# Output products of a two-stage layer: operand sums made inside the plain group, a last evacuation deferred, tiles padded

## The chip, the core and the metric

The kernel runs on one core of a Trainium2 chip. The metric is the device time of one execution in microseconds (us). Five engines matter: TensorE (PE; its weight loads are the row PEld), VectorE (DVE), ScalarE (ACT), GpSimd (POOL), and SyncE (SP), which issues the DMAs. Each works through its own list of instructions in order; a semaphore wait on the first one holds up all behind it.

## The reference

The input x has 512 tokens of 2048 features, all float32. One layer of a gated recurrence (HGRN2), then one of forgetting attention (FoX), each with a gate path and an output product added to the stream:

```
def hgrn2_layer(x, norm_w, w_in, lb, out_norm_w, w_out):
    h = rmsnorm(x, norm_w)
    proj = h @ w_in
    ...
    o = o.reshape(B, T, D_MODEL) * jax.nn.silu(gate.astype(jnp.float32))
    return x + (o.astype(x.dtype) @ w_out)
```

The attention layer ends in the same way: the branch times silu(gate), a product with a 2048 x 2048 matrix, and the residual. These two output products are what the change is about.

## The kernel before

Everything is kept transposed: a tile is 128 features by 512 tokens, and a 2048-wide operand is 16 contraction tiles (kt). Every product is made from operands split into a high part (a cast on ScalarE, line L432) and a low part (a subtraction on DVE, L433), with three matmuls: high by high, high by low, low by high.

**A plain group** (group, L205) makes four output tiles in four PSUM banks gm: for each kt it takes one weight tile wh, wl (128 x 512) and issues 4 x 3 matmuls of 512 columns (L227 to L229, with Xh and Xl moving; in the token-major form L223 to L225 the weights move and x is stationary). Weights come by DMA in chunks of 512 KB (tile wr, two buffers, two kt each). At each kt, group splits the weights of the next kt ahead of the matmuls; at the last kt that is the first weight of the *next* group. In stages A and B, split weights have three buffers, in the output stages two (w_tiles, L124).

**A quick group** (quick, L254) makes two output tiles of 512 tokens with seven products where eight would be needed, a Strassen-Winograd scheme: for each of eight pairs p of contraction tiles it issues seven products of 256 columns, three matmuls each (L282 to L284). Both operands then need sums: those of the weights (w_sums, L142, tile wm, DVE L146 to L148) for each weight chunk, and those of the input (quick_prep, L239), made once for all six quick groups of a stage. For a pair, quick_prep takes four quarters of two y tiles, makes three differences on DVE (L244, L246, L247) and one on POOL (L245) in the single buffer tm, and splits them: one over the upper half of Xh[p], Xl[p] (256 columns), three into th, tl (768 columns). The upper half of Xh[p] may be overwritten only when the plain group has read it. quick_sum (L287) takes the seven products apart: one ScalarE copy (L291), seven DVE operations (L292 to L301), and the result is stored, squared and added to the norm's sum (x1_done, ScalarE L346, POOL L347).

**The stages.** a: sixteen plain groups (order_a, the last is g3), with the recurrence's small tasks in between; oa: the output product, one plain group for output tiles 0 to 3 and six quick groups u0 to u5 for the other twelve; b and ob likewise, the first group of b is q0. A gate group ends with gate_evac (L374): for each of four banks a DVE product z (L378), on ScalarE Abs, Exp, Ln and Exp (L364 to L366, L381), on DVE L367, on POOL z times t (L382), on DVE y times z (L384). y is the input of the output product and is split per kt (y_split) as xh, xl.

**Pools.** Each stage has its own tile pool (phase, L67), all laid over the same addresses, so a tile of a new stage waits for the last readers of what lay there. Which instruction stands where in an engine's list is set by a scheduler that goes by the order of the program's lines and a timeline of its own; the lists shown below are its result.

**What surrounds the change.** out_product (L823) runs the plain group first, still in the pool of the old stage with three weight buffers: while g3's last contraction tiles are on TensorE, its first weights are already split. Only at its last kt are the remaining tasks flushed and the new phase opened; the sums of pairs 0 to 3 are then issued, those of 4 to 7 inside u0. Pair p is the contraction tiles p and p + 8. After oa's u5 its evacuation is issued at once, then phase b is opened, the small forget-gate weights wf, wfs are made (L852 to L858), and q0 begins, whose x1_split (L846) splits the rows of x1 one kt after the other.

Of the kernel before, what the change touches and what calls it, by code (L numbers as in the profile page):

```python
# [1 line left out]

# [29 lines left out]
def hgrn2_fox(ctx, tc, io):  # L32
# [10 lines left out]

    def nt(tag, shape, bufs, dt=F32, pool=None):
        uid[0] += 1
        return (pool or sb).tile(list(shape), dt, tag=tag, name=f"{tag}_{uid[0]}", bufs=bufs)

    def const(tag, shape, dt=F32):
        return cp.tile(list(shape), dt, tag=tag, name=tag)

    def view(t, offset, dims):
        return bass.AP(t.tensor, t.offset + offset, [t.ap[0], *dims])
# [7 lines left out]
    def bank():  # L60
        return nt("mx", (P, T), 4, pool=ps)
# [96 lines left out]
    class Chunks:  # L158
# [43 lines left out]
        Xl[kt] = nt(f"xl{kt}", (P, T), 1, F32R)  # L202
        return Xh[kt], Xl[kt]

    def group(evac, token_major=False, rate=3, before=None):  # L205

        banks = [nt(f"gm{j}", (P, T), 1, pool=ps) for j in range(4)]
        for kt in range(KT):
            if kt % 2 == 0:
                wts.load()  # L210
            if before:
                before(kt)
            if not wts.parts:
                wts.split()
            h, l = wts.take()
            if not wts.parts:
                wts.split()
            for j in range(4):
                c = slice(j * P, (j + 1) * P)
                f, e = kt == 0, kt == KT - 1  # L220
                if token_major:
                    xh, xl = Xh[kt][:, c], Xl[kt][:, c]
                    PE.matmul(banks[j], xh, h, start=f, stop=False)  # L223
                    PE.matmul(banks[j], xh, l, start=False, stop=False)  # L224
                    PE.matmul(banks[j], xl, h, start=False, stop=e)  # L225
                else:
                    PE.matmul(banks[j], h[:, c], Xh[kt], start=f, stop=False)  # L227
                    PE.matmul(banks[j], h[:, c], Xl[kt], start=False, stop=False)  # L228
# [9 lines left out]

    def quick_prep(p, y):  # L239

        kt = p + KT // 2
        b11, b12, b21, b22 = y[p][:, :TN], y[p][:, TN:], y[kt][:, :TN], y[kt][:, TN:]
        m = mt("tm", (P, 4, TN), 1)
        V.tensor_sub(m[:, 0, :], b12, b11)  # L244
        G.tensor_sub(m[:, 2, :], b12, b22)  # L245
        V.tensor_sub(m[:, 1, :], b22, m[:, 0, :])  # L246
        V.tensor_sub(m[:, 3, :], b21, m[:, 1, :])  # L247
        th = mt(f"th{p}", (P, 3, TN), 1, F32R)
        tl = mt(f"tl{p}", (P, 3, TN), 1, F32R)
        split(m[:, 0, :], Xh[p][:, TN:], Xl[p][:, TN:])  # L250
        split(m[:, 1:4, :], th, tl)
        return th, tl

    def quick(banks, prep, evac, before=None):  # L254

        half = lambda i: banks[i // 2][:, (i % 2) * TN : (i % 2 + 1) * TN]
        for p in range(KT // 2):
            if p % 2 == 0:
                wts.load()
# [12 lines left out]
            for i, (a, xh, xl) in enumerate((
                (2, Xh[p][:, lo], Xl[p][:, lo]),
                (5, th[:, 0, :], tl[:, 0, :]),
                (1, th[:, 2, :], tl[:, 2, :]),
                (3, Xh[p][:, hi], Xl[p][:, hi]),
                (0, Xh[kt][:, lo], Xl[kt][:, lo]),
                (6, Xh[kt][:, hi], Xl[kt][:, hi]),
                (4, th[:, 1, :], tl[:, 1, :]),
            )):  # L280
                o = half(i)
                PE.matmul(o, h[:, a, :], xh, start=f and i % 2 == 0, stop=False)  # L282
                PE.matmul(o, h[:, a, :], xl, start=False, stop=False)
                PE.matmul(o, l[:, a, :], xh, start=False, stop=e and (i % 2 == 1 or i == 6))  # L284
        evac(*banks)

    def quick_sum(r1, r2, o1, o2, p16, p45, p23, p7):  # L287

# [11 lines left out]
        V.tensor_add(o1, e, r1)  # L300
        V.tensor_add(o2, d, r2)  # L301

    def quick_groups(y, residual, evac):

        prep = [quick_prep(p, y) for p in range(4)]

        def run():
            for u in range(6):
                k = 4 + 2 * u
                r = [residual(k), residual(k + 1)]  # L310
                banks = [nt(f"gm{j}", (P, T), 1, pool=ps) if u % 2 == 0 else bank() for j in range(4)]
                quick(
                    banks, prep, lambda *p, k=k, r=r: evac(k, r, p),
                    before=(lambda p: p < 4 and prep.append(quick_prep(4 + p, y))) if u == 0 else None,
                )

        return run


    def sum_parts(x, out_bank):  # L320
# [13 lines left out]
    class Norm:  # L334
# [15 lines left out]
        def finish(self):  # L350
            b = bank()
            sum_parts(self.acc, b)
            self.row = nt("rstd", (P, T), 1)
            rsqrt_mean(self.row, b, D)
            b2 = bank()
            for w in range(NW):
                PE.transpose(b2[:, w * P : (w + 1) * P], self.row[:, w * P : (w + 1) * P], ident)
            self.col = nt("rstdc", (P, NW, 1), 1)
            V.tensor_copy(self.col, b2.rearrange("p (w c) -> p w c", c=P)[:, :, 0:1])


# [9 lines left out]
    def gate_evac(norm, h0):  # L371
        def evac(j, bk):
            h = h0 + j
            new = Y[h] is None  # L374
            if new:
                Y[h] = nt(f"y{h}", (P, T), 1)
            z = Y[h] if new else nt("z", (P, T), 4)
            V.tensor_mul(z, bk, norm.row)  # L378
            l = tmp()
            log_sigmoid(l, z, l)  # L380
            S.activation(l, l, AF.Exp)  # L381
            G.tensor_mul(z, z, l)  # L382
            if not new:
                V.tensor_mul(Y[h], Y[h], z)  # L384

        return evac
# [373 lines left out]
    for name in order_a:  # L760
        kind, i = name[0], int(name[1])
        before = load_x if name == order_a[0] else None
        if kind == "q":
            group(qf_evac(2 * i), before=before, rate=RATE_A)
            tasks.append((2 * i, mix_a(2 * i)))
            tasks.append((2 * i + 1, mix_a(2 * i + 1)))
        elif kind == "v":
            group(v_evac(norm0, 4 * i), token_major=True, rate=RATE_A)
        else:
            group(gate_evac(norm0, 4 * i), rate=RATE_A)  # L770

# [80 lines left out]
    wf = mt("t", (P, KT, H), 4)  # L852
    nc.sync.dma_start(wf, io["wb_f"])
    wfs = mt("wfs", (P, KT, 48), 1, F32R)
    V.memset(wfs.bitcast(F32), 0.0)
    V.tensor_mul(wf, wf, view(nk, 0, [[1, KT], [0, H]]))
    V.tensor_copy(wfs[:, :, 0:H], wf)
    V.tensor_sub(wfs[:, :, 32 : 32 + H], wf, rd(wfs)[:, :, 0:H])  # L858
    f_d = dr.tile([H, T], F32, tag="fd", name="fd")

    def forget():
# [108 lines left out]
    for name in order_b:  # L970
        kind, i = name[0], int(name[1])
        if kind == "q":
            group(qk_evac(2 * i), before=x1_split if first else None, rate=RATE_B)
            if first:
                forget()
            first = False
            tasks.append((2 * i, mix_b(2 * i)))
            tasks.append((2 * i + 1, mix_b(2 * i + 1)))
        elif kind == "v":
            group(v_evac(norm1, 4 * i), token_major=True, rate=RATE_B)  # L980
        else:
            group(gate_evac(norm1, 4 * i), rate=RATE_B)

    def res_b(kt):
        r = nt("z", (P, T), 4)
# [14 lines left out]
        for i in range(2):  # L1000
            nc.sync.dma_start(io["out"][k + i], r[i])

    out_product(out_b_evac(), res_b, quick_b, RATE_B, "ob")
    cur["ctx"].close()


# [75 lines left out]
```

## Time and profile before

| quantity | value |
|---|---|
| time, median of 3 runs | 2089.97 us (2087.96 to 2094.06) |
| time of the profiled execution | 2092.97 us |
| its span, first to last instruction | 2091.2 us |
| mean granted TensorE clock | 0.989 |
| TensorE busy | 2028.2 us, 97% |
| VectorE busy | 1579.0 us, 76% |
| ScalarE busy | 1132.6 us, 54% |
| GpSimd busy | 316.1 us, 15% |
| DMA | 195.01 MB, mean 93 GB/s |

How to read the rows that follow. A row of stretches gives from:to in us, its length, then for each engine the busy time and the count of instructions, the mean granted TensorE clock (1.00 is full), the busy share of the DMA engines and GB/s. A row of waits gives who waits for whom, the total in us, how often, and the longest. A row of a tile or a line gives the count and durations in ns. A timeline row gives start, duration, engine, line, operation, output <- inputs, and in brackets how long the engine was idle before it and what ended that. The duration of a matmul includes its way through the array; how fast they follow each other is seen from their starts or their count in a stretch. Line numbers are those of the kernel before.

### The profile page before, as it was taken

To read this page: it belongs to the slowest core of one execution; us is meant where nothing else is said; L and a number is where in the kernel's file an instruction comes from. 1 tells how busy PE (TensorE), PEld (TensorE's weight loads), DVE (VectorE), ACT (ScalarE), POOL (GpSimd) and SP (SyncE) were. 2 spreads that over 40 slices of the span, in tenths; PEclk is the share of its full clock that TensorE was granted. 3 is DMA by queue.
4 is the path that set the end of the run, shared out by engine and by line. 5 is a ranking of instruction groups with operands and counts; after the bars stand their busy time and mean duration, and the time that the engine had idled before them with its cause. 6 is when DMAs were issued, how large, how long until landed. Compare 5 with 4: busy or idle time off the path is not lost.

```text
span 2091.2 us, 28900 instructions
## 1 busy us (share of the span) xinstructions
PE 2028.2 (97%) x10202; PEld 1701.7 (81%) x10202; DVE 1579.0 (76%) x3250; ACT 1132.6 (54%) x2312; POOL 316.1 (15%) x404
## 2 busy tenths in 40 slices
PE   7999999999999999988989999999999999999798
PEld 5888888888888888768977888888888888888698
DVE  8778977988799788769884667665766666685887
ACT  5646655666566465634443555554555556564343
POOL 7303210322132031211210000010001000011100
PEclk9999999999999999989999999999999999999899
DMA  5222222222222222233533232223222222223353
GB/s 172 81 81 81 71 81 71 81 81 71 81 71 81 76 76 71 90 117 117 161 104 91 87 95 91 86 78 99 91 86 87 91 91 86 86 82 109 101 165 108
DMA packets 61408, 195.01 MB, mean 93 GB/s; under 512 B 7872, under 2 KB 8000, under 8 KB 61264
## 3 DMA queue, kind: packets, MB, share of 16 engines
q1 hardware_dynamic: 61120, 193.17, 29.5%
q8 instruction: 80, 1.31, 0.3%
q14 instruction: 64, 0.52, 0.1%
q10 hardware_dynamic: 144, 0.01, 0.0%
HBM read 184.73 MB, written 8.42 MB: 92 GB/s over the span
## 4 chain that ended last, share of the span: by engine, by line
PE 83%; DVE 7%; DMA 3%; ACT 2%; issue 2%; POOL 2%; SPq 0%; DVEq 0%; ACTq 0%; POOLq 0%
PE gm L227 17%; PE gm L229 17%; PE gm L228 17%; PE gm L224 5%; PE gm L223 5%; PE gm L225 5%; DVE wl L433 3%; DMA wr<-in_wb_q 2%; PE mx L580 1%; PE mx L579 1%; PE mx L578 1%; PE mx L427 1%; PE mx L428 1%; PE mx L284 1%; PE mx L426 1%
## 5 line engine op out<-in xcount | busy, mean ns | idle before, releaser
L227 PE MATMUL gm<-xh,wh 128*128 128x512 f32 x1664 | 662.0, 398 | 13.9 <-ACT wh L432 8.3
L228 PE MATMUL gm<-xl,wh 128*128 128x512 f32 x1664 | 661.8, 398 | 0.0
L229 PE MATMUL gm<-xh,wl 128*128 128x512 f32 x1664 | 625.6, 398 | 5.7 <-DVE wl L433 5.5
L227 PEld LDWEIGHTS gm<-xh,wh 128*128 128x128 f32 x1664 | 314.3, 189 | 86.5 <-ACT wh L432 8.3
L229 PEld LDWEIGHTS gm<-xh,wl 128*128 128x128 f32 x1664 | 312.1, 189 | 77.6 <-DVE wl L433 7.0
L228 PEld LDWEIGHTS gm<-xl,wh 128*128 128x128 f32 x1664 | 314.5, 189 | 71.6
L432 ACT CAST wh<-wr 128x512 fp32r<-128x512 f32 (+1 forms) x336 | 217.3, 649 | 232.5 <-PE gm L228 125.8
L433 DVE TENSOR_TENSOR wl<-wr,wh 128x512 fp32r<-128x512 f32 (+1 forms) x336 | 261.8, 783 | 107.7 <-ACT wh L432 101.5
L138 DVE SCALAR_TENSOR_TENSOR wl<-wr,v_b_norm_w,wh 128x256 fp32r<-128x256 f32 (+1 forms) x192 | 113.7, 594 | 152.1 <-ACT wh L137 141.2
L137 ACT ACTIVATE wh<-wr,v_b_norm_w 128x256 fp32r<-128x256 f32 (+1 forms) x192 | 111.9, 586 | 196.8 <-PE gm L228 155.9
L224 PE MATMUL gm<-wl,xh 128*128 128x512 f32 x512 | 203.7, 398 | 0.4 <-DVE wl L433 0.4
L225 PE MATMUL gm<-wh,xl 128*128 128x512 f32 x512 | 202.1, 396 | 0.0
L223 PE MATMUL gm<-wh,xh 128*128 128x512 f32 x512 | 185.8, 396 | 0.0
L137 ACT ACTIVATE wh<-wr,v_kv_norm_w 128x256 fp32r<-128x256 f32 (+1 forms) x192 | 110.3, 575 | 63.2 <-PE gm L225 46.2
L138 DVE SCALAR_TENSOR_TENSOR wl<-wr,v_kv_norm_w,wh 128x256 fp32r<-128x256 f32 (+1 forms) x192 | 111.2, 580 | 38.6 <-ACT wh L137 38.0
L924 POOL TENSOR_SCALAR_AFFINE_SELECT s<-s 128x128 f32<-128x128 f32 x64 | 27.4, 428 | 669.7 <-DVE s L923 669.0
L573 DVE COPY_PREDICATED at<-m,mx 128x128 f32<-128x128 uint8 (+3 forms) x448 | 106.6, 296 | 13.6 <-PE mx L580 13.0
L223 PEld LDWEIGHTS gm<-wh,xh 128*128 128x128 f32 x512 | 95.9, 188 | 22.4 <-DVE q L544 0.2
L224 PEld LDWEIGHTS gm<-wl,xh 128*128 128x128 f32 x512 | 96.2, 188 | 21.5 <-DVE wl L433 0.9
L225 PEld LDWEIGHTS gm<-wh,xl 128*128 128x128 f32 x512 | 96.1, 188 | 20.9
L432 ACT CAST kh<-k 128x512 fp32r<-128x512 f32 (+1 forms) x96 | 56.4, 587 | 52.0 <-PE mx L579 25.8
L382 POOL TENSOR_TENSOR z<-z,t 128x512 f32<-128x512 f32 x32 | 47.9, 1509 | 237.0 <-ACT t L381 236.9
(217 smaller groups left out, 3893.9 us busy)
## 6 DMA issues: line engine op xcount, KB each, us to landing
wr<-in_wa_qf SPq DMA_DIRECT2D x64, 512.0 KB, 3.6
wr<-in_wb_qk SPq DMA_DIRECT2D x64, 512.0 KB, 3.5
wr<-in_wa_v SPq DMA_DIRECT2D x32, 512.0 KB, 3.5
wr<-in_wa_g SPq DMA_DIRECT2D x32, 512.0 KB, 3.5
wr<-in_wb_v SPq DMA_DIRECT2D x32, 512.0 KB, 3.5
wr<-in_wb_g SPq DMA_DIRECT2D x32, 512.0 KB, 3.5
wr<-in_wa_q SPq DMA_DIRECT2D x24, 512.0 KB, 3.6
wr<-in_wb_q SPq DMA_DIRECT2D x24, 512.0 KB, 3.6
```

Of the source, the lines that this page charges most:

```text
L137: S.activation(h[:, c], r[:, c], AF.Copy, scale=w[:, kt : kt + 1])
L138: V.scalar_tensor_tensor(l[:, c], r[:, c], w[:, kt : kt + 1], rd(h)[:, c], op0=ALU.mult, op1=ALU.subtract)
L223: PE.matmul(banks[j], xh, h, start=f, stop=False)
L224: PE.matmul(banks[j], xh, l, start=False, stop=False)
L225: PE.matmul(banks[j], xl, h, start=False, stop=e)
L227: PE.matmul(banks[j], h[:, c], Xh[kt], start=f, stop=False)
L228: PE.matmul(banks[j], h[:, c], Xl[kt], start=False, stop=False)
L229: PE.matmul(banks[j], l[:, c], Xh[kt], start=False, stop=e)
L382: G.tensor_mul(z, z, l)
L432: S.copy(h, src)
L433: return V.tensor_sub(l, src, rd(h))
L573: V.copy_predicated(out, mv, data)
```

## The change

Four things are altered.

1. **The output stages** open their phase before the plain group instead of at its last kt. The sums of a pair are made inside the plain group, as soon as both of its y tiles have been split, that is after each odd kt.
2. **Pairs** are neighbouring contraction tiles, 2p and 2p + 1, instead of p and p + 8; the host lays the weights of the quick groups out accordingly. The count of instructions on each engine stays the same.
3. **hold** keeps the last gate group of a stage, and u5 of oa, from splitting the first weight of the following group. quick returns its evacuation as a function; oa's last one is called inside q0 at its third kt, and the forget-gate weights are made at its seventh.
4. **Padding**: a tile whose rows aren't a multiple of 64 bytes is made longer, so that every tile begins at a multiple of 64 bytes. Before, all tiles of the stages' pools began 32 bytes beyond one; xh, xl, y, z and wr lie in another pool that began at a multiple already. A small tile (rstdc) goes to the pool of constants.

```
     def quick_prep(p, y):
-        kt = p + KT // 2
-        b11, b12, b21, b22 = y[p][:, :TN], y[p][:, TN:], y[kt][:, :TN], y[kt][:, TN:]
+        k1, k2 = 2 * p, 2 * p + 1
+        b11, b12, b21, b22 = y[k1][:, :TN], y[k1][:, TN:], y[k2][:, :TN], y[k2][:, TN:]
...
-    def out_product(evac0, residual, evac, rate, name):
-
-        rest = []
+    def out_product(evac0, residual, evac, name, hold):
+
+        flush()
+        phase(name)
+        prep = []
 
         def before(kt):
             y_split(kt)
-            if kt == KT - 1:
-                flush()
-                phase(name)
-                rest.append(quick_groups(Yd, residual, evac))
-
-        group(evac0, before=before, rate=rate)
-        rest[0]()
-
-    out_product(out_a_evac(), res_a, quick_a, RATE_A, "oa")
+            if kt % 2:
+                prep.append(quick_prep(kt // 2, Yd))
+
+        group(evac0, before=before)
+        return quick_groups(prep, residual, evac, hold)
+
+    last_a = out_product(out_a_evac(), res_a, quick_a, "oa", True)
...
     def x1_split(kt):
+        if kt == 2:
+            last_a()
+        if kt == 6:
+            forget_weights()
...
-            if not wts.parts:
+            if not (wts.parts or hold and kt == KT - 1):
                 wts.split()
...
-        b = w.reshape(2, 8, P, n, 2, P).transpose(3, 1, 2, 0, 4, 5)
+        b = w.reshape(8, 2, P, n, 2, P).transpose(3, 0, 2, 1, 4, 5)
```

What that does to the engines' lists, at three places. In the changed kernel the lines of group, quick and the splits lie some further down (L432 is L435, L227 is L237, L378 is L381, L364 to L366 are L367 to L369, L381 is L384, L384 is L387). The numbers behind a name tell buffers apart.

**ScalarE, from the end of g3 into oa's plain group, before.** wh_9232 and wh_9323 are the plain group's weights of kt 0 and 1, t the gate activations of g3's last evacuation:

```order
L432 CAST wh_9216<-wr_9180 128x512 [waits DVE_50,PE_50]
L432 CAST wh_9232<-wr_9214 128x512 [waits DMAHW1_50,DVE_50,PE_50]
L432 CAST wh_9323<-wr_9214 128x512 [waits DVE_50,PE_50]
L364 ACTIVATE t_9241<-z_9239 128x512 [waits DVE_50]
L432 CAST wh_9343<-wr_9317 128x512 [waits DMAHW2_50,PE_50,Activation_50]
L364 ACTIVATE t_9254<-z_9252 128x512 [waits DVE_50]
L365 ACTIVATE t_9241<-t_9241 128x512 [waits Activation_50]
```

The weights go ahead of the activations. **The same place after the change;** here wh_9323 and wh_9327 are kt 0 and 1:

```order
L369 ACTIVATE t_9276<-t_9276 128x512 [waits Activation_50]
L384 ACTIVATE t_9250<-t_9250 128x512 [waits DVE_50]
L384 ACTIVATE t_9263<-t_9263 128x512 [waits DVE_50]
L384 ACTIVATE t_9276<-t_9276 128x512 [waits DVE_50]
L435 CAST xh_1878_9641<-y_1426_7294 128x512 [waits DVE_50,PE_50]
L435 CAST xh_1882_9661<-y_1502_7684 128x512 [waits DVE_50,PE_50]
L435 CAST xh_1890_9694<-y_1619_8290 128x512 [waits DVE_50,PE_50]
L435 CAST wh_9323<-wr_9214 128x512 [waits DMAHW1_50,Pool_50]
L435 CAST wh_9327<-wr_9214 128x512 [waits PE_50]
```

All sixteen activations and the casts of y tiles 12 to 14 now stand ahead of the first weight, and that waits for POOL: its buffer lies over t_9276, which POOL reads in its last product. Stage ob has the same pattern.

**DVE, inside oa's plain group, after the change.** wl are low weights, tm, tl and the 256-wide xl belong to the sums (before, this stretch held low weights and xl only):

```order
L436 TENSOR_TENSOR xl_1819_9377<-tm_9400,xh_1818_9376 128x256 [waits Activation_50]
L254 TENSOR_TENSOR tm_9453<-y_622_3138 128x256 [waits DVE_50]
L256 TENSOR_TENSOR tm_9453<-y_698_3528,tm_9453 128x256 [waits DVE_50]
L257 TENSOR_TENSOR tm_9453<-y_698_3528,tm_9453 128x256 [waits DVE_50]
L436 TENSOR_TENSOR wl_9434<-wr_9374,wh_9433 128x512 [waits PE_50,Activation_50]
L436 TENSOR_TENSOR tl_1838_9459<-tm_9453,th_1837_9458 128x768 [waits Activation_50]
L436 TENSOR_TENSOR wl_9465<-wr_9427,wh_9464 128x512 [waits DMAHW0_50,PE_50,Activation_50]
```

Two low weights and five operations of a pair take turns, the low weights waiting for TensorE to free a buffer.

**ScalarE, from u5 into q0, before** (L291 is the last evacuation's copy, L346 its squares, wh_11191 and wh_11261 the weights of kt 0 and 1):

```order
L137 ACTIVATE wh_11191<-wr_11168,v_kv_norm_w 128x256
L432 CAST wh_11141<-wm_11137 128x2x512 [waits DVE_50]
L432 CAST xh_2116_11395<-y_1960_10242 128x512 [waits PE_50]
L291 COPY t_11220<-mx_11002 128x512 [waits PE_50]
L432 CAST xh_2120_11417<-y_1961_10243 128x512 [waits PE_50]
L346 ACTIVATE z_11232<-y_2075_11218 128x512 [waits DMAHW6_50,DVE_50]
L432 CAST xh_2152_11579<-y_2075_11218 128x512
L346 ACTIVATE z_11236<-y_2076_11219 128x512 [waits DVE_50,Pool_50]
L137 ACTIVATE wh_11261<-wr_11168,v_b_norm_w 128x256
```

The second weight of q0 comes behind the squares of the evacuation. **And after,** with wh_11228, wh_11234 and wh_11256 for kt 0, 1 and 2:

```order
L147 ACTIVATE wh_11228<-wr_11168,v_b_norm_w 128x256 [waits DMAHW7_50,Activation_50]
L147 ACTIVATE wh_11228<-wr_11168,v_kv_norm_w 128x256
L147 ACTIVATE wh_11234<-wr_11168,v_b_norm_w 128x256 [waits DVE_50,PE_50]
L147 ACTIVATE wh_11234<-wr_11168,v_kv_norm_w 128x256
L147 ACTIVATE wh_11256<-wr_11222,v_b_norm_w 128x256 [waits DMAHW0_50]
L147 ACTIVATE wh_11256<-wr_11222,v_kv_norm_w 128x256
L299 COPY t_11278<-mx_11002 128x512
L147 ACTIVATE wh_11301<-wr_11222,v_b_norm_w 128x256 [waits DVE_50,PE_50]
```

Three weights precede the copy, and DVE has the matching three wl ahead of its part of the evacuation.

More of the change, by code (lines that the diff above doesn't have):

```diff
@@ L45, in nt, with padded @@
         uid[0] += 1
-        return (pool or sb).tile(list(shape), dt, tag=tag, name=f"{tag}_{uid[0]}", bufs=bufs)
+        return padded(pool or sb, shape, dt, tag, f"{tag}_{uid[0]}", bufs)
+    def padded(pool, shape, dt, tag, name, bufs=1):
+        n = math.prod(shape[1:])
+        unit = 64 if dt == U8 else 16
+        if n % unit == 0:
+            return pool.tile(list(shape), dt, tag=tag, name=name, bufs=bufs)
+        t = pool.tile([shape[0], -(-n // unit) * unit], dt, tag=tag, name=name, bufs=bufs)[:, :n]
+        return t.rearrange("p (a b) -> p a b", b=shape[2]) if len(shape) == 3 else t
     def const(tag, shape, dt=F32):
-        return cp.tile(list(shape), dt, tag=tag, name=tag)
+        return padded(cp, shape, dt, tag, tag)
     def view(t, offset, dims):
@@ L203, in new_x, with group @@
         return Xh[kt], Xl[kt]
-    def group(evac, token_major=False, rate=3, before=None):
+    def group(evac, token_major=False, rate=3, before=None, hold=False):
         banks = [nt(f"gm{j}", (P, T), 1, pool=ps) for j in range(4)]
@@ L249, in quick_prep, with quick @@
         tl = mt(f"tl{p}", (P, 3, TN), 1, F32R)
-        split(m[:, 0, :], Xh[p][:, TN:], Xl[p][:, TN:])
+        split(m[:, 0, :], Xh[k1][:, TN:], Xl[k1][:, TN:])
         split(m[:, 1:4, :], th, tl)
         return th, tl
-    def quick(banks, prep, evac, before=None):
+    def quick(banks, prep, evac, hold):
         half = lambda i: banks[i // 2][:, (i % 2) * TN : (i % 2 + 1) * TN]
@@ L264, in quick @@
             h, l = wts.take()
-            if not wts.parts:
+            if not (wts.parts or hold and p == KT // 2 - 1):
                 wts.split()
             th, tl = prep[p]
-            kt = p + KT // 2
+            k1, k2 = 2 * p, 2 * p + 1
             lo, hi = slice(0, TN), slice(TN, T)
@@ L301, in quick_sum, with quick_groups @@
         V.tensor_add(o2, d, r2)
[L303 to L317, printed above, removed]
+    def quick_groups(prep, residual, evac, hold):
+        for u in range(6):
+            k = 4 + 2 * u
+            r = [residual(k), residual(k + 1)]
+            banks = [nt(f"gm{j}", (P, T), 1, pool=ps) if u % 2 == 0 else bank() for j in range(4)]
+            end = quick(banks, prep, lambda *p, k=k, r=r: evac(k, r, p), hold and u == 5)
+            if u < 5:
+                end()
+        return end
     def sum_parts(x, out_bank):
@@ L769, in hgrn2_fox @@
         else:
-            group(gate_evac(norm0, 4 * i), rate=RATE_A)
+            group(gate_evac(norm0, 4 * i), rate=RATE_A, hold=name == order_a[-1])
     Yd = [None] * KT
@@ L849, in x1_split, with forget_weights @@
             norm1.finish()
-    wf = mt("t", (P, KT, H), 4)
-    nc.sync.dma_start(wf, io["wb_f"])
     wfs = mt("wfs", (P, KT, 48), 1, F32R)
[L855 to L858, printed above, removed]
+    def forget_weights():
+        wf = mt("t", (P, KT, H), 4)
+        nc.sync.dma_start(wf, io["wb_f"])
+        V.memset(wfs.bitcast(F32), 0.0)
+        V.tensor_mul(wf, wf, view(nk, 0, [[1, KT], [0, H]]))
+        V.tensor_copy(wfs[:, :, 0:H], wf)
+        V.tensor_sub(wfs[:, :, 32 : 32 + H], wf, rd(wfs)[:, :, 0:H])
     f_d = dr.tile([H, T], F32, tag="fd", name="fd")
@@ L981, in hgrn2_fox @@
         else:
-            group(gate_evac(norm1, 4 * i), rate=RATE_B)
+            group(gate_evac(norm1, 4 * i), rate=RATE_B, hold=name == order_b[-1])
     def res_b(kt):
```

17 lines of the change are left out of this document (8 added, 9 removed).

## Prediction

> **What bounds the kernel now.** I read the page first, then the busy time by stretches, cut where the stages of the output products begin and end, then the waits inside the worst stretch, and last the instructions in order of time at the two handovers.
>
> ```profile
> span 2091.2 us, 28900 instructions
> PE   7999999999999999988989999999999999999798
> core 0: us, PE busy (x) PEld busy (x) DVE busy (x) ACT busy (x) POOL busy (x), PEclk, DMA share, GB/s
> 828.90:875.20 46.30, 46.30 (x204) 37.48 (x204) 32.40 (x54) 26.86 (x50) 6.56 (x4) 1.00 0.31 94
> 875.20:921.40 46.20, 44.83 (x193) 35.80 (x192) 25.66 (x36) 20.78 (x37) 7.44 (x5) 1.00 0.36 114
> 921.40:986.60 65.20, 51.35 (x346) 47.70 (x345) 58.97 (x93) 27.66 (x38) 16.11 (x12) 0.84 0.34 112
> 986.60:1025.60 39.00, 39.00 (x330) 38.92 (x329) 34.85 (x54) 18.08 (x22) 12.19 (x4) 1.00 0.47 149
> 1025.60:1077.70 52.10, 45.78 (x349) 43.82 (x348) 44.63 (x66) 24.85 (x36) 5.69 (x4) 0.97 0.39 122
> 1895.70:1940.50 44.80, 44.80 (x193) 36.08 (x193) 23.15 (x32) 20.88 (x37) 8.20 (x5) 1.00 0.37 116
> 1940.50:2024.20 83.70, 69.94 (x505) 65.63 (x505) 75.50 (x124) 33.03 (x43) 7.57 (x7) 0.92 0.40 126
> 2024.20:2064.90 40.70, 40.16 (x338) 39.96 (x338) 35.01 (x57) 15.88 (x18) 0.00 (x0) 1.00 0.47 157
> ```
>
> TensorE is the limit nearly everywhere. The slices below 9 are the start, the end, and the two output products: slices 18 to 21 are stage oa and its exit, 37 and 38 stage ob. Only there can a change of order gain anything.
>
> The rows are, for oa: the last gate group before it, its plain group, the first two quick groups u0 and u1, then u2 and u3, u4 and u5. For ob: plain group, u0 to u2, u3 and u4. Undisturbed, a plain group's 192 matmuls take 44.8 us (0.232 each), and 330 matmuls of 256 columns 39.0 us (0.118), so that a quick group of 168 takes 19.8 us. By that, u0 and u1 should take 39.6 us and take 65.2: 25.6 us lost. The plain group of oa loses 46.2 - 44.6 = 1.6 us. In ob, u0 to u2 take 83.7 us for 59.4: 24.3 us lost. Some of each loss is idle time (65.20 - 51.35 = 13.9 us in oa), the rest is the clock that the idle time brings down (0.84 and 0.92). What ends the idle time in u0 and u1:
>
> ```profile
> PE gm L282 <- ACT th L432: 5.7, 3, 3.1
> PE gm L282 <- ACT wh L432: 3.3, 1, 3.3
> PE gm L282 <- DVE y L811: 2.3, 1, 2.3
> ACT th L432 <- DVE tm L247: 10.4, 6, 2.5
> ```
>
> TensorE waits for the operand sums th, ScalarE for DVE's share of them (tm). DVE is busy 58.97 of 65.2 us: it makes sums, splits, weight sums and evacuations at once. In the plain group just before, it is busy 25.66 of 46.2. So the work is in the wrong place, and the change moves it to the right one.
>
> **The change part by part.** *The sums go from u0 into the plain group.* They cost, all 16 pairs of the two stages together:
>
> ```profile
> L245 POOL TENSOR_TENSOR tm<-y,y x16: 857/977/1725, 887.9 to 1983.4; 128x256 f32<-128x256 f32 x16
> L244 DVE TENSOR_TENSOR tm<-y x16: 410/424/957, 914.2 to 1983.4; 128x256 f32<-128x256 f32 x16
> L246 DVE TENSOR_TENSOR tm<-y,tm x16: 409/836/846, 918.5 to 1983.8; 128x256 f32<-128x256 f32 x16
> L432 ACT CAST xh<-tm x16: 403/406/408, 918.6 to 1983.8; 128x256 fp32r<-128x256 f32 x16
> L247 DVE TENSOR_TENSOR tm<-y,tm x16: 409/412/419, 922.9 to 1985.8; 128x256 f32<-128x256 f32 x16
> L432 ACT CAST th<-tm x16: 829/832/838, 923.4 to 1986.4; 128x768 fp32r<-128x768 f32 x16
> L433 DVE TENSOR_TENSOR tl<-tm,th x16: 947/957/1360, 924.3 to 1987.2; 128x768 fp32r<-128x768 f32 x16
> ```
>
> The other terms are in the timelines of DVE and ScalarE at the handover from the gate group to oa, which also serve the next step (start, duration, instruction):
>
> ```profile
> 872.77 0.69 DVE L433 TENSOR_TENSOR wl<-wr,wh 128x512 fp32r<-128x512 f32 x1 [2.11 <-ACT wh L432]
> 883.24 1.78 DVE L384 TENSOR_TENSOR y<-y,z 128x512 f32<-128x512 f32 x1
> 884.94 3.45 DVE L433 TENSOR_TENSOR wl<-wr,wh 128x512 fp32r<-128x512 f32 x2
> ```
> ```profile
> 874.10 0.64 ACT L364 ACTIVATE t<-z 128x512 f32<-128x512 f32 x1 [1.36 <-DVE z L378]
> 874.96 0.62 ACT L432 CAST wh<-wr 128x512 fp32r<-128x512 f32 x1 [0.23 <-PE gm L228]
> 876.02 0.62 ACT L365 ACTIVATE t<-t 128x512 f32<-128x512 f32 x1
> 876.55 0.61 ACT L364 ACTIVATE t<-z 128x512 f32<-128x512 f32 x1
> ```
>
> A pair is two contraction tiles, 24 matmuls, 24 x 0.232 = 5.57 us of TensorE. DVE has 0.42 + 0.84 + 0.41 + 0.96 for the sums, some 0.41 for the low half of xl (as the other 256-column operations), and two weight splits at 0.69: 4.4 us. ScalarE has 0.41 + 0.83 + 2 x 0.62 = 2.5 us, POOL 0.98. All fit within 5.57. There are waits inside: two wh and wl buffers only, and the casts into the upper half of Xh[2p] must wait until TensorE has read contraction tile 2p, with the next weight split queued behind them on ScalarE and DVE. A wh buffer is free after the eighth matmul of its contraction tile and wanted 16 matmuls (3.7 us) later; 0.62, or 1.9 with th and xh in front, fits. I price steady stalls in the group at nothing, covered by these 3.7 us; without the cover see the first rival. At the first weights of u0, which still come behind the last sums and the squares and adds of the plain group's evacuation, I allow 2 us per stage.
>
> *The weights of the plain group wait for the new phase.* This is the price of moving the phase forward. Before, the first weight casts ran while the last gate group was still on TensorE. Now wh of contraction tile 0 stands behind all sixteen activations of the last gate evacuation, three xh casts, and the last POOL product, over whose operand t its buffer lies.
>
> ```profile
> 881.47 6.37 POOL L382 TENSOR_TENSOR z<-z,t 128x512 f32<-128x512 f32 x4 [23.43 <-ACT t L381]
> ```
>
> ScalarE's pitch is 0.53 us (876.02 to 876.55). No weight split stands before z any more: z of the first bank starts when that bank is done, nine matmuls before the end, and the first activation at about 873.8 instead of 874.10. The eleventh (the first L381) then ends near 879.7, the sixteenth near 882.3. POOL multiplies from 879.8, 6.4 us for four: done at 886.2. DVE's products y follow each of them and take up to 1.78 us beside POOL: the third ends about 887.2, its xh cast 887.8, wh 888.4. TensorE ends the gate group at 875.2, so it stands still for 13.2 us. If DVE is not slowed by POOL, wh ends at 886.8 and the gap is 11.6; if one more POOL instruction (1.6 us) comes into its way, the gap is 14.8. After 13.9 us idle in pieces the clock was at half for 20 us in all (0.84 of 65.2); here the idle time is one piece, and the one piece of 4.72 us below cost 1.7 us by the clock. I take 2.5 us, ends 1.7 and twice that. In ob the row of POOL is like that of oa (8.20 us for the same five instructions against 7.44): 13.4 us and 2.5.
>
> A rule on this: by the Trainium skill (TensorE: Matmul & The Clock Gate, Part 1: The HAM clock gate) an idle window of about 3.4 us halves the array's clock until a busy one has passed. It speaks against two new gaps of 13 us; the trace agrees in kind (0.84 in the stretch with 13.9 us of gaps), and by the rule alone the restart would cost about 1.7 us, not my 2.5.
>
> Sums. Oa: 25.6 + 1.6 lost now, 13.2 + 2.5 + 2 = 17.7 lost then, **9.5 us gained**. Ob: 24.3 lost now, 13.4 + 2.5 + 2 = 17.9 then, **6.4 gained**.
>
> *The last evacuation of oa is deferred into q0.*
>
> ```profile
> 1076.27 0.59 ACT L291 COPY t<-mx 128x512 f32<-128x512 f32 x1 [0.33 <-PE mx L284]
> 1080.61 0.63 ACT L346 ACTIVATE z<-y 128x512 f32<-128x512 f32 x1 [3.00 <-DVE y L300]
> 1082.18 0.49 ACT L137 ACTIVATE wh<-wr,v_b_norm_w 128x256 fp32r<-128x256 f32 x1
> 1082.73 0.79 PE L227 MATMUL gm<-xh,wh 128*128 128x512 f32 x1 [4.72 <-ACT wh L137]
> ```
> ```profile
> 1078.00:1100.00 22.00, 17.28 (x69) 13.93 (x69) 16.09 (x31) 9.02 (x20) 2.88 (x2) 0.92 0.40 126
> ```
>
> Now ScalarE waits at L346 for six DVE operations of the evacuation, and the second weights of q0 stand behind it: TensorE idles 4.72 us. In the changed order three pairs of weight casts precede the evacuation on ScalarE, and three wl on DVE. Their buffers lie where u5's last weights lay, so the first wl has to wait for u5's last matmul; it then takes two operations, 0.9 us, and TensorE has eight matmuls of contraction tile 0, 1.86 us, that need only wh. So the gap closes. I take 4.7, and 1.7 for the clock (0.92 over 22 us is 3.5 us at half speed): **6.4 us gained**. What is late next is u5's own low weights: 52.1 - 39.6 - 2.8 (twelve matmuls of q0 that ran inside) = 9.7 us are lost in u4 and u5, and I leave them.
>
> *Padding.* It moves addresses from 32 to 0 beyond a multiple of 64 bytes. Which matmul operands start on such a multiple now can be told from the pools: Xh and Xl do, the weights and the sums don't.
>
> ```profile
> L227 PE MATMUL gm<-xh,wh 128*128 128x512 f32 x1664 | 662.0, 398 | 13.9 <-ACT wh L432 8.3
> L223 PE MATMUL gm<-wh,xh 128*128 128x512 f32 x512 | 185.8, 396 | 0.0
> ```
>
> L227 streams Xh past wh, L223 streams wh past Xh, and the two take the same 396 to 398 ns. I price padding at nothing.
>
> Sum: 9.5 + 6.4 + 6.4 = **22.3 us**, from the profiled execution's 2092.97 to 2070.7. That execution lies 3.0 above the median of 2089.97, so against the median **2067.7 us**.
>
> **The rivals.** *The plain group becomes DVE's (slower).* With POOL's subtraction now in the group in each pair, and every wait in DVE's order, all of a pair could run at the long ends: 0.96 + 0.85 + 0.42 + 1.36 + 0.41 + 3.45 (two wl, the row above) = 7.45 us per pair against 5.57. That is 1.88 x 16 = 30 us, and the sum turns to 7.8 us slower, 2097.8. It decides from 22.3 / 16 = 1.4 us over per pair, that is 6.97. For it: L246's median is twice its minimum. Against it: POOL works 1 us of each pair's 5.57, so not all five can meet it. 12%. The Trainium skill (SBUF — State Buffer, Who interferes with whom) has a DVE instruction with two SBUF inputs and a GpSimd one that reads SBUF lock each other out; the 1.78 us of the row above beside POOL is in keeping with it, and by that rule a pair would lose about one POOL instruction, and still fit.
>
> *The deferral only shifts the gap.* If the first wl of q0 comes after the evacuation or its buffer late, TensorE stops there: the 6.4 us stay, 2074. The order speaks against it. 10%.
>
> *Given back later.* u2 to u5 have DVE busy 34.85 of 39.0 us and 44.63 of 52.1: if u0 and u1 go at 19.8 us each, their evacuations and weights crowd DVE there; the 9.7 us in u4 and u5 could double, 2077. 10%.
>
> *Nothing measurable.* The gaps ahead of the plain groups are worked out, not seen: 18 us each instead of 13 take 10 us back, and a deferral that only shifts its gap 6.4 more: 2084. Against it: the chain of rows that ends at wh has room for one POOL instruction, not for three. 9%.
>
> *Faster matmuls by padding.*
>
> ```profile
> 958.32 0.41 PE L284 MATMUL gm<-th,wl 128*128 128x256 f32 x1
> 958.53 0.41 PE L282 MATMUL gm<-xh,wh 128*128 128x256 f32 x1
> ```
>
> At half clock 256 columns take 0.213 us (two starts, to the rounding), half of which is 0.107, not the 0.118 of the full clock. If it were the addresses that take these 9%, some 1900 us of matmuls would shrink by 170 us, to about 1900. Against it: L227 and L223 above, equal whichever operand is off. None of before has both on, so it stays possible: 4%. The Trainium skill (TensorE: Matmul & The Clock Gate, Wait — 56ns, not 53.3ns?) gives 215.7 ns for 512 columns on the warm array; the trace has 232.
>
> **How the numbers follow.** The forecast has 55%, the rivals 12, 10, 10, 9 and 4. Left out of the range are the first and the last, 16%. Its lower end: gaps of 11.6 and 11.8, 1.7 for each restart and no 2 us, 9 us together, and half of u4's and u5's stalls, 5: 2053. The upper end is the no-change case, 2087. About 0.3%, 6.3 us, is what a measurement can tell from no change: faster below 2083.7. Faster: 55 + 10 + 10 + 4, less 1 for the forecast's edge = 78%; within: 10%; slower: the first rival, 12%.
>
> **What would show it.** After the change: the 44.8 us plain groups have one gap of about 13 us ahead of their first matmul, waiting for wh, and no more than 1 us of gaps inside; u0 and u1 take 40 to 42 us together; the first weight split of q0 has no gap before it; u2 to u5 as now. I am wrong if the gap ahead is over 18 us, if pairs take over 7 us, or if u2 to u5 grow.

## The result, and the profile after

The changed kernel takes 2057.68 us (median of 4 runs, 2056.82 to 2059.76) against 2090.59 us: ratio 0.9843, 95% interval 0.9826 to 0.9860, some 33 us less. The forecast was 2067.7, in a range from 2053 to 2087. Sign and range were right; that the time comes near the sum is luck, since two of its parts were wrong, as the stages show. The page after, first its head, the slices, then two of the matmul groups:

```profile
span 2055.4 us, 28924 instructions
PE 1986.9 (97%) x10202; PEld 1696.2 (83%) x10202; DVE 1585.9 (77%) x3250; ACT 1133.1 (55%) x2312; POOL 305.6 (15%) x404
PE   7999999999999999889999999999999999997998
L237 PE MATMUL gm<-xh,wh 128*128 128x512 f32 x1664 | 654.2, 393 | 37.6 <-ACT wh L435 36.5
L233 PE MATMUL gm<-wh,xh 128*128 128x512 f32 x512 | 183.6, 392 | 0.3 <-DVE q L547 0.2
```

The busy time of TensorE fell by 41 us with the same count of matmuls, and one matmul of 512 columns shows 392 to 393 ns where it showed 396 to 398. That is not what waits look like. L237 has 36.5 us of waiting for wh, against 8.3 before. The stretches, cut like those of before (gap ahead of oa's plain group, the group, its quick groups, the first matmuls of q0; then the gap, the group and the quick groups of ob):

```profile
866.30:881.10 14.80, 0.16 (x1) 0.00 (x0) 11.65 (x13) 10.05 (x20) 7.13 (x5) 0.65 0.16 38
881.10:929.20 48.10, 45.27 (x192) 37.04 (x193) 38.88 (x66) 22.05 (x37) 6.22 (x7) 0.96 0.36 109
929.20:1063.90 134.70, 128.54 (x1007) 125.47 (x1008) 119.75 (x167) 60.59 (x80) 20.80 (x13) 0.96 0.44 141
1063.90:1068.00 4.10, 4.10 (x21) 3.41 (x20) 4.03 (x11) 2.99 (x7) 0.00 (x0) 1.00 0.23 52
1861.40:1875.70 14.30, 0.24 (x2) 0.00 (x0) 10.44 (x14) 10.75 (x22) 6.40 (x5) 0.59 0.14 40
1875.70:1924.80 49.10, 46.25 (x192) 37.73 (x192) 38.92 (x66) 22.04 (x35) 6.22 (x7) 0.95 0.35 106
1924.80:2049.00 124.20, 123.59 (x1007) 122.65 (x1008) 98.13 (x154) 44.89 (x51) 0.00 (x0) 0.99 0.45 145
```

The same from the trace of before, where it was not shown yet (all quick groups of oa, the step into q0, all quick groups of ob):

```profile
921.40:1077.70 156.30, 136.13 (x1020) 130.44 (x1019) 138.45 (x210) 70.59 (x96) 33.98 (x20) 0.92 0.39 124
1077.70:1082.70 5.00, 0.31 (x3) 0.10 (x1) 4.89 (x9) 2.09 (x5) 1.27 (x1) 0.96 0.26 96
1940.50:2084.80 144.30, 130.00 (x1008) 125.41 (x1008) 123.19 (x199) 55.06 (x68) 7.57 (x7) 0.95 0.39 128
```

| stretch | before, us | after, us | difference |
|---|---|---|---|
| stage a, to the end of g3 | 875.2 | 866.3 | -8.9 |
| oa with the step into q0 (less 2.8 us of q0 that ran inside it before) | 46.2 + 156.3 + 5.0 - 2.8 = 204.7 | 14.8 + 48.1 + 134.7 = 197.6 | -7.1 |
| stage b, from there to the end of its last group | 815.8 | 797.5 | -18.3 |
| ob, plain and quick groups | 44.8 + 144.3 = 189.1 | 14.3 + 49.1 + 124.2 = 187.6 | -1.5 |

The spans differ by 35.8 us; 27.2 of it lie in stages a and b, where the forecast had nothing, and 8.6 in the output stages, where it had 22.3. The quick groups did gain, 153.5 - 134.7 = 18.8 us in oa and 20.1 in ob, and the step of 5.0 us into q0 went, but the plain groups with the gaps ahead of them lost 16.7 and 18.6.

The gap ahead of oa's plain group, in the timelines of TensorE, POOL and ScalarE:

```profile
881.16 0.80 PE L237 MATMUL gm<-xh,wh 128*128 128x512 f32 x1 [14.71 <-ACT wh L435]
```
```profile
872.87 4.72 POOL L385 TENSOR_TENSOR z<-z,t 128x512 f32<-128x512 f32 x3 [0.29 <-ACT t L384]
```
```profile
865.18 1.31 ACT L367 ACTIVATE t<-z 128x512 f32<-128x512 f32 x2 [6.45 <-DVE z L381]
879.97 0.62 ACT L435 CAST xh<-y 128x512 fp32r<-128x512 f32 x1 [1.12 <-DVE y L387]
880.49 1.13 ACT L435 CAST wh<-wr 128x512 fp32r<-128x512 f32 x2
```

The order of steps is the forecast's: activations from 865.18, POOL to 877.6, the third y, its xh cast at 879.97, then wh. POOL, over whose operand t the buffer of wh lies, was done 2.9 us before wh began; what held wh last was its place behind the xh cast, which waited for y. In ob, POOL and ScalarE show the same (the buffer of the first wh doesn't lie over t there, which sets right the "same pattern" said of ob above):

```profile
1871.34 2.64 POOL L385 TENSOR_TENSOR z<-z,t 128x512 f32<-128x512 f32 x2 [3.43 <-ACT t L384]
```
```profile
1874.56 0.62 ACT L435 CAST xh<-y 128x512 fp32r<-128x512 f32 x1 [2.84 <-DVE y L387]
1875.08 1.14 ACT L435 CAST wh<-wr 128x512 fp32r<-128x512 f32 x2
```

What TensorE waited for from the gap to the start of u0, in oa and then in ob:

```profile
PE gm L237 <- ACT wh L435: 14.7, 1, 14.7
PE gm L290 <- DVE y L814: 2.8, 1, 2.8
```
```profile
PE gm L237 <- ACT wh L435: 14.1, 1, 14.1
PE gm L290 <- DVE z L1003: 2.8, 1, 2.8
```

No third wait stands there: inside the plain groups, sixteen pairs of sums went by without a stall.

### The profile page after: what moved, and what is told of

The parts are those of the page before. It is cut to its first block, busy times and chain, and to the rows that moved or that the text cites. A ratio compares the mean times of both kernels' runs of the same rounds, so it can differ in the third digit from the quotient of the medians.

```text
span 2055.4 us, 28924 instructions
## 1 busy us (share of the span) xinstructions
PE 1986.9 (97%) x10202; PEld 1696.2 (83%) x10202; DVE 1585.9 (77%) x3250; ACT 1133.1 (55%) x2312; POOL 305.6 (15%) x404
## 4 chain that ended last, share of the span: by engine, by line
PE 74%; DVE 13%; DMA 4%; issue 3%; ACT 3%; POOL 2%; SPq 0%; DVEq 0%; ACTq 0%; POOLq 0%
PE gm L237 16%; PE gm L239 16%; PE gm L238 16%; PE gm L234 5%; PE gm L233 5%; PE gm L235 5%; DVE wl L436 3%; DMA wr<-in_wa_q 2%; DMA wr<-in_wb_q 2%; PE mx L583 1%; PE mx L581 1%; PE mx L582 1%; DVE ml L436 1%; PE mx L430 1%; PE mx L431 1%
## 5 line engine op out<-in xcount | busy, mean ns | idle before, releaser
L237 PE MATMUL gm<-xh,wh 128*128 128x512 f32 x1664 | 654.2, 393 | 37.6 <-ACT wh L435 36.5
L238 PE MATMUL gm<-xl,wh 128*128 128x512 f32 x1664 | 653.5, 393 | 0.0
L239 PE MATMUL gm<-xh,wl 128*128 128x512 f32 x1664 | 605.8, 393 | 6.0 <-DVE wl L436 5.5
L237 PEld LDWEIGHTS gm<-xh,wh 128*128 128x128 f32 x1664 | 314.7, 189 | 102.9 <-ACT wh L435 37.6
L435 ACT CAST wh<-wr 128x512 fp32r<-128x512 f32 (+1 forms) x336 | 217.4, 650 | 217.6 <-PE gm L238 114.8
L436 DVE TENSOR_TENSOR wl<-wr,wh 128x512 fp32r<-128x512 f32 (+1 forms) x336 | 257.5, 770 | 75.5 <-ACT wh L435 60.7
L148 DVE SCALAR_TENSOR_TENSOR wl<-wr,v_kv_norm_w,wh 128x256 fp32r<-128x256 f32 (+1 forms) x192 | 112.2, 586 | 35.8 <-ACT wh L147 35.3
L435 ACT CAST kh<-k 128x512 fp32r<-128x512 f32 (+1 forms) x96 | 56.5, 588 | 52.3 <-PE mx L582 19.2
```

The source lines that it names most:

```text
L148: V.scalar_tensor_tensor(l[:, c], r[:, c], w[:, kt : kt + 1], rd(h)[:, c], op0=ALU.mult, op1=ALU.subtract)
L435: S.copy(h, src)
L436: return V.tensor_sub(l, src, rd(h))
```

## The experiments

Two theories at the start. **A**: the addresses of the tiles set TensorE's pace, and with it stages a and b. **B**, that of the prediction: addresses cost nothing, and the order of the output stages gives the gain. Ratios are to the kernel before in the same runs.

**Padding alone.**

```
-        return (pool or sb).tile(list(shape), dt, tag=tag, ...)
+        return padded(pool or sb, shape, dt, tag, ...)
...
-            self.col = nt("rstdc", (P, NW, 1), 1)
+            self.col = nt("rstdc", (P, NW, 1), 1, pool=cp)
```

> The kernel before with the padding alone: every tile starts at a multiple of 64 bytes, the order of all engines is that of before. Theory A, addresses set TensorE's pace: stages a and b take what they take in the changed kernel, 9.1 and 18.5 us less than before, and the stages of the output products win about 1 us on each plain group and lose about 1 us on the quick groups of each stage (118 to 120 ns a matmul): about 2063 us. Theory B, the one on record, padding costs and gains nothing and a and b were quicker for another reason: 2090 us.

2065.26 us, ratio 0.9872 (0.9857 to 0.9887): 27 us less, with the engines' order of before. B is out.

**The rest of the change alone.** The changed kernel with nt, const and rstdc as before.

```
-        return padded(pool or sb, shape, dt, tag, f"{tag}_{uid[0]}", bufs)
+        return (pool or sb).tile(list(shape), dt, tag=tag, name=f"{tag}_{uid[0]}", bufs=bufs)
```

> The changed kernel without the padding: sums in the plain group, new pairs, hold, deferred evacuation, on the old addresses. If addresses set the pace of TensorE (27.6 us of the 35.7 by which the span fell lie in stages a and b, which the rest of the change doesn't touch), this is 2082 to 2086 us, with a and b as long as before. If the order of the output stages gives the gain as the prediction had it, 2068 us.

2085.01 us, ratio 0.9969 (0.9957 to 0.9982): 6.5 us less. The two halves add up, by the ratios: 26.8 + 6.5 = 33.3 us for 32.8 measured with both.

**Which addresses.** Three kernels without any padding: only rstdc, 16 bytes per partition at the end of the pool of x, moved to the pool of constants; or 32 bytes put ahead of all pools; or both.

```
-            self.col = nt("rstdc", (P, NW, 1), 1)
+            self.col = const("rstdc", (P, P // 8))[:, :NW].rearrange("p (w c) -> p w c", c=1)
```
```
+    G.memset(const("filler", (P, 8)), 0.0)
     eps = const("eps", (P, 1))
```

> The kernel before with one small tile (rstdc) moved to the pool of constants and 64 bytes given to it there, so that the stages' pools start at a multiple of 64 bytes; no tile is padded, and tiles that come behind the odd small ones still lie 32 bytes off. Xh, Xl, wh and wl are all at multiples of 64 (of 128 none). Theory A: if the operands of the large matmuls are what counts, the same as with full padding, about 2063 us; if multiples of 128 are needed, 2090; if the small and the attention tiles count too, in between. Theory B: 2090 us.

> The kernel before with 32 bytes put ahead of all pools: Xh, Xl, y, z and the raw weights move to 32 bytes off a multiple of 64, the stages' pools with wh and wl onto a multiple; that is the reverse of before. A first form of theory A, both operands must start on a multiple of 64: 2090 us, a pace of 232 to 235 ns per 512 columns. A second form, only the tiles of the stages' pools (weights) count: about 2063 us and 227 ns. Theory B: 2090 us.

> The kernel before with all of it, both x and the weights, 32 bytes off a multiple of 64. Theory A, both must be on a multiple: 2090 us or more. Theory A in a third form, what counts is that both operands stand at the same offset: about 2063 us, 227 ns per 512 columns. Theory B: 2090 us.

Measured: 2065.45 us, ratio 0.9875 (0.9858 to 0.9891), for rstdc alone; 2091.68, 1.0001 (0.9990 to 1.0011), for the filler alone, with x off and the weights on a multiple of 64, still 32 apart; 2063.33, 0.9866 (0.9846 to 0.9886), with both 32 bytes off. So it isn't alignment. What counts is that x and the weights lie at the same offset, and moving one tile of 16 bytes gives all of the padding's gain: the tiles in the pool of x are 57 times 2048 bytes, and rstdc behind them shifted the stages' pools by 32.

**Same offset within how much.** Full padding, and a filler at the head of each stage's pool, another size in each stage, in two kernels.

```
+        off = {"a": 16, "oa": 24, "b": 32, "ob": 64}[name]
+        G.memset(cur["sb"].tile([P, off], F32, tag="off", name=f"off{name}"), 0.0)
```
```
+        off = {"a": 128, "oa": 256, "b": 96, "ob": 192}[name]
```

> The kernel before with full padding, and a filler at the start of each stage's pool, so that the weights start at another offset to x in each stage: 64 bytes in a, 96 in oa, 128 in b, 256 in ob (x stays at a multiple of 2048; in the runs so far the offset was 0, which was fast, or 32, which was slow). If only the offset within 64 bytes counts, a, b and ob run at 227 ns per 512 columns and oa at 232 to 235: about 2066 us. If the offset must be a multiple of 128 (256), a runs at 232 to 235 too (a and b): about 2075 (2092). Theory on record, no effect of addresses, is out by now.

> As the kernel with a filler in each stage's pool, with other sizes: the weights start 512 bytes off x in a, 1024 in oa, 384 in b, 768 in ob. Offsets 32, 64, 96, 128 and 256 were slow, 0 fast. If a multiple of 512 is what counts, a and oa run at 227 ns per 512 columns, b and ob at 232 to 235, and the time is 2090 less the 9 us that stage a gained: 2081 to 2084 us. If only the offset 0 within 2048 is fast, all four are slow: 2090.

Measured: 2089.84 us, ratio 0.9987 (0.9976 to 0.9997), and 2082.71, 0.9955 (0.9936 to 0.9975). How fast matmuls follow each other in a group of stage a, from two starts ten matmuls apart, 64 bytes off and then 512 bytes off:

```profile
299.90 0.39 PE L240 MATMUL gm<-xl,wh 128*128 128x512 f32 x1
302.23 0.39 PE L241 MATMUL gm<-xh,wl 128*128 128x512 f32 x1
```
```profile
299.90 0.39 PE L241 MATMUL gm<-xh,wl 128*128 128x512 f32 x1
302.17 0.39 PE L240 MATMUL gm<-xl,wh 128*128 128x512 f32 x1
```

233 ns, and 227. In stage b, the matmuls in the same 50 us, for before (32 off), the changed kernel (0), both 32 off (0 between them), the first kernel with fillers (128) and the second (384), one fence each:

```profile
1400.00:1450.00 50.00, 50.00 (x216) 40.28 (x215) 32.69 (x63) 25.90 (x55) 2.86 (x2) 1.00 0.33 105
```
```profile
1400.00:1450.00 50.00, 50.00 (x227) 41.43 (x226) 34.95 (x76) 27.19 (x61) 1.35 (x4) 1.00 0.32 100
```
```profile
1400.00:1450.00 50.00, 50.00 (x227) 41.48 (x226) 32.36 (x72) 25.15 (x56) 0.88 (x3) 1.00 0.31 96
```
```profile
1400.00:1450.00 50.00, 50.00 (x216) 40.23 (x215) 32.79 (x62) 24.68 (x52) 2.85 (x2) 1.00 0.34 102
```
```profile
1400.00:1450.00 50.00, 50.00 (x219) 40.38 (x219) 31.05 (x66) 22.13 (x49) 1.30 (x3) 1.00 0.30 95
```

TensorE is busy all through, at a clock of 1.00, in each; only the count differs (the windows don't start at the same matmul, so two or three are noise).

Which distances that tests needs care. In these two kernels the engines' order is that of before, so the plain groups of oa and ob still take their weights from the pools of a and b, and nearly all matmuls of 512 columns ran at the distances of those two stages. By the starts, their median in each stage is 227 ns at 0 and 512 bytes, and 232 to 235 at 32, 64, 128 and 384. The distances 96, 256, 768 and 1024 lie in the pools of oa and ob, where the matmuls have 256 columns; for 512 columns the runs don't show them, though the second expectation counts 96 and 256 as slow. So a multiple of 512 bytes is fast, and whether 256 would be isn't shown. The four banks' slices of one weight tile lie 512 bytes apart, which is why one offset serves them all.

Matmuls of 256 columns go the other way: 120 ns in the quick groups with the weights 0, 256, 768 or 1024 bytes off x, 118.5 at 32 and 96. Here the distance of a matmul's own operands isn't shown as the cause: th and tl lie in the weights' pool, and in the trace of before their matmuls take 118.5 ns, like those of xh and xl.

**Without the deferral.** The changed kernel with oa's last evacuation at once and no hold at u5.

```
-    last_a = out_product(out_a_evac(), res_a, quick_a, "oa", True)
+    out_product(out_a_evac(), res_a, quick_a, "oa", False)()
...
-        if kt == 2:
-            last_a()
-        if kt == 6:
-            forget_weights()
```

> The changed kernel with the last evacuation of oa made at once and without hold at u5, as before the change, and the forget-gate weights made ahead of q0. If the deferral is worth what the prediction had, a gap of about 4.7 us and half a clock window come back ahead of the second contraction tile of q0: 2064 us. If it is worth nothing because something else is late there, 2058 us.

2063.39 us, ratio 0.9863 (0.9848 to 0.9878) against 0.9843: 4.2 us by the ratios, 5.7 by the medians. The two intervals overlap, so the trace has to decide. The gap is back, ahead of q0's second contraction tile (timeline of TensorE, then of ScalarE):

```profile
1070.26 0.50 PE L237 MATMUL gm<-xh,wh 128*128 128x512 f32 x1 [3.63 <-ACT wh L147]
```
```profile
1068.14 0.63 ACT L349 ACTIVATE z<-y 128x512 f32<-128x512 f32 x1 [3.54 <-DVE y L308]
1069.72 0.49 ACT L147 ACTIVATE wh<-wr,v_b_norm_w 128x256 fp32r<-128x256 f32 x1
```

In the 22 us behind it the granted clock is 0.92, where the changed kernel has 1.00 there: 1.8 us more, 5.4 in all.

**The new phase later.** The phase at the fifth contraction tile, the last gate group without hold:

```
-        flush()
-        phase(name)
         prep = []
 
         def before(kt):
             y_split(kt)
-            if kt % 2:
-                prep.append(quick_prep(kt // 2, Yd))
+            if kt == 4:
+                flush()
+                phase(name)
+            while kt > 4 and len(prep) < (kt + 1) // 2:
+                prep.append(quick_prep(len(prep), Yd))
```

> The changed kernel with the new phase opened at the fifth contraction tile of the plain group instead of before it, the last gate group splitting the first plain weight again (no hold there), and the sums of pairs 0 to 2 made at the sixth contraction tile, the others as in the changed kernel. Theory: the 14.7 and 14.1 us ahead of the plain groups are there because everything of a new phase stands behind the last instruction of the old one; weights that stay in the old pool go ahead of the gate activations. Then both gaps go, with their half clock (1.5 and 2.6 us): 2057.7 - 33 = 2025 us, or up to 8 us more if the sixth weight still waits for POOL or DVE has three pairs at once. Rival: the activations hold ScalarE in any order, and the gaps only move into the plain group: 2050 us or more.

2038.37 us, ratio 0.9743 (0.9729 to 0.9758): 19 us less than the changed kernel, not 33. The waits of TensorE from g3's end to u0, in oa:

```profile
PE gm L290 <- DVE y L814: 3.1, 1, 3.1
PE gm L237 <- ACT wh L435: 2.5, 1, 2.5
PE gm L239 <- DVE wl L436: 1.6, 1, 1.6
```

14.7 us of waiting for wh became 2.5, now at the sixth contraction tile; in ob 14.1 became 2.6. ScalarE's timeline in oa shows the weights of the old pool among the activations, and the first of the new pool still behind the xh casts:

```profile
865.76 0.62 ACT L435 CAST wh<-wr 128x512 fp32r<-128x512 f32 x1
873.07 1.13 ACT L435 CAST wh<-wr 128x512 fp32r<-128x512 f32 x2
874.10 1.15 ACT L384 ACTIVATE t<-t 128x512 f32<-128x512 f32 x2
882.79 0.62 ACT L435 CAST xh<-y 128x512 fp32r<-128x512 f32 x1 [0.59 <-DVE y L387]
883.31 1.13 ACT L435 CAST wh<-wr 128x512 fp32r<-128x512 f32 x2
```

So the gaps come from the order in the list, in oa as in ob, and not from the buffer over t, which the prediction named beside it. The rest of the 33 us stayed, in part in the waits above and as longer waits for wl in oa's quick groups (6.8 us for 4.9). The half clock stayed too: behind the waits that are left, of 2.5 to 3.1 us, 15.9 us ran at a clock of 0.50 (from 884.0, 918.9, 1870.4 and 1904.6), against 14.2 us at the same places of the changed kernel, behind gaps of up to 14.7.

**The phase one later, and other banks for u0 in ob.**

```
-            if kt == 4:
+            if kt == 5:
...
-            while kt > 4 and len(prep) < (kt + 1) // 2:
+            while kt > 5 and len(prep) < (kt + 1) // 2:
...
-            banks = [nt(f"gm{j}", (P, T), 1, pool=ps) if u % 2 == 0 else bank() for j in range(4)]
+            banks = [nt(f"gm{j}", (P, T), 1, pool=ps) if u % 2 != hold else bank() for j in range(4)]
```

> The kernel that opened the phase at the fifth contraction tile, with two further edits: the phase opens at the sixth, so that the first weight behind it is wanted 2.7 us later, and in ob the first quick group takes the four banks that the plain group did not use. Theory: of the gaps left there, 2.5 and 2.6 us inside the two plain groups come from the weight behind the old pool's last POOL instruction, and go; 2.5 us and half a clock window (1.7) ahead of u0 in ob come from banks that wait for DVE's evacuation, and go too: 2038.4 - 5.1 - 2 x 1.7 - 2.5 - 1.7 = 2026 us. Rivals: the later sums crowd DVE ahead of u0, and the gaps move there: 2034 to 2038; the banks of u1 wait instead of those of u0: 2030 us.

2030.30 us, ratio 0.9709 (0.9693 to 0.9725), the fastest here and 27 us below the changed kernel; 4 us short of what was expected. The waits in oa, and then in ob from g3's end into u0:

```profile
PE gm L290 <- DVE y L814: 3.2, 1, 3.2
PE gm L239 <- DVE wl L436: 1.6, 1, 1.6
PE gm L237 <- ACT wh L435: 0.4, 1, 0.4
```
```profile
PE mx L290 <- ACT wh L435: 2.0, 1, 2.0
PE gm L237 <- ACT wh L435: 1.6, 1, 1.6
PE mx L292 <- DVE wl L436: 0.7, 1, 0.7
```

In ob the wait for the banks (2.8 in the changed kernel) is gone, and u0's second weight chunk is late by 2.0 instead: the first rival in that expectation, in part. The second rival gave 2030 us too, but its wait isn't there: from u0 to the end of ob TensorE waits for wh and wl alone. The wait of 1.6 us for wh in ob's plain group is left, and the clock is 1.00 behind it.

## Why the prediction was right and wrong

*Padding at nothing.* This is the step that failed, and the largest term: 26.8 us by the run with padding alone. The other step is the size of the gain in the output stages: 22.3 us forecast, 6.5 by the run without padding. That the measured time came near the forecast at all is owed to the term that the sum had at nothing, and is luck. The rows on which the prediction rested for padding, L227 and L223 at 398 and 396 ns, were read as "equal whichever operand is off". But both have one operand of each kind, 32 bytes apart; exchanging their roles keeps the distance, so the pair could not show what distance costs. The rival "faster matmuls by padding", at 4% and 170 us, had the direction right; alignment as its cause was wrong, and the size was 27 us. What it argued from, 0.118 us for 256 columns against 0.107 worked out from the half clock, is another matter: with padding those matmuls take 0.120.

*What limits the rest of the pace stays open.* The best medians are 227 ns for 512 columns and 120 for 256. They differ by 107 ns for 256 columns, and by that rate each takes some 13 ns longer than its columns alone. The Trainium skill (TensorE: Matmul & The Clock Gate, Wait — 56ns, not 53.3ns?) gives 215.7 ns for 512 columns at the full clock; no run here reached it. The Trainium skill (SBUF — State Buffer, Who interferes with whom) calls TensorE's two read ports, one for the moving operand and one for weights, independent; that the distance of the two operands in memory changes the pace (227 ns against 232 to 235) doesn't follow from that, and these runs don't show the mechanism.

*The gaps ahead of the plain groups.* 13.2 and 13.4 us were worked out, 14.7 and 14.1 measured, from the same chain of steps. POOL was done 11.1 us after the gate group's end, for 11.0 worked out; the third y came 1.4 us late, behind a low half xl that took 1.21 us beside POOL's next instruction. That is close to the 14.8 that the prediction gave for one more POOL instruction in the way. The clock: 0.96 over 48.1 us and 0.95 over 49.1 are 3.8 and 4.9 us at half speed, 1.9 and 2.5 us lost, for 2.5 each. Half of the reason given, the buffer over t, was not what held the weights, as the two timelines and the run with a later phase show.

*The sums in the plain group.* Right: no stall inside, u0 and u1 in 42.2 us, just over the 40 to 42 forecast, and the slower rival (DVE sets the pace of pairs) did not come.

```profile
929.20:971.40 42.20, 42.14 (x337) 41.80 (x338) 37.89 (x52) 18.32 (x23) 8.03 (x5) 0.97 0.48 152
971.40:1063.90 92.50, 86.39 (x673) 83.67 (x672) 81.86 (x116) 42.27 (x57) 12.77 (x8) 0.96 0.42 137
```

*2 us at u0.* 2.8 us in each stage, and 1.4 and 1.7 us more by the clock behind it (0.87 from 929.2 to 940.0, 0.83 from 1924.8 to 1934.8), for another cause than named: u0 takes the banks that the plain group has just filled and waits for DVE to empty them (y L814, z L1003).

*Given back later.* u2 to u5 of oa took 92.5 us, against 39.0 + 52.1 - 2.8 = 88.3 before. That they grow is one of the signs of being wrong that the prediction set itself. But the stalls it feared did not grow: TensorE idles 6.1 us of the 92.5, and idled 6.3 of the 52.1 before. About 1 us is the slower pace of 256 columns (672 x 1.4 ns), 0.7 that the stretch holds six matmuls more, and some 2 the clock (0.96 over 92.5 us loses 3.7, 0.97 over 52.1 lost 1.6). This rival had 10% and came to 4 us, but not by its cause.

*The deferral.* 6.4 us forecast, 4.2 to 5.7 by the times and 5.4 by the trace; the gap was closed as described.

*In sum.* By the stretches the output stages gave 8.6 us for 22.3, 13.7 short. The gaps ahead were 1.6 and 0.9 longer than taken (14.8 and 14.3). The plain groups, with the clock and the stall at u0, were 1.0 and 0.2 shorter (48.1 and 49.1 for 49.1 and 49.3), since their matmuls run at 227 ns now. The quick groups were 6.8 and 4.2 longer: 134.7 for 39.6 + 39.0 + 52.1 - 2.8 = 127.9, and 124.2 for 120.0. Of that about 1.4 in each stage is the pace of 256 columns, and 1.4 and 1.7 the clock after the stall at u0; in oa another 3.2 is what u2 to u5 gave back beside the pace, in ob 0.6 is idle time. Under 1 us in each is left without a cause. The last 1.4 us are the clock after the old gap at q0, which lies behind these stretches. Nearly every term fell on the same side, and the 26.8 us that the sum had at nothing covered them.

## What to carry to other kernels

Two rows that differ in several things at once, or keep the one thing fixed that the change alters, price nothing: ask of a row whether it would have looked different if the effect existed. To see whether addresses cost anything, move one pool by a few bytes and count the operations in a stretch that is busy all through. And when a second experiment moves another tile, check which pool the measured operands lie in. If a stage's first loads or casts belong to a new pool, see what of the old pool stands ahead of them in each engine's list; keeping the first few in the old pool was worth more than the change that moved the pool.

## What the runs showed of the hardware

Matmuls of 512 columns in this float32 form follow each other every 227 ns when moving and stationary operand lie 0 or 512 bytes apart in a partition, and every 232 to 235 ns at 32, 64, 128 and 384, the four other distances that these runs show; the absolute position (0, 64 or 96 bytes off a multiple of 128) made no difference. For 256 columns it is 120 ns with the weights 0, 256, 768 or 1024 bytes off x, and 118.5 at 32 and 96, for a cause that stays open.

A wait of TensorE of 2.5 us cost about as much clock as one of 14.7: behind each, 3.0 to 3.3 us ran at half (884.0 to 887.3 with the later phase, 881.2 to 884.2 in the changed kernel); behind the 14.1 of ob it was 5.1. Behind waits of 1.6 us in the fastest kernel it stayed at 1.00.
